# Five more pairs with seven products, other lead lengths, and sums of x beside the last latent heads in a hybrid encoder layer

## The chip, the cores and the metric

The kernel runs on one core of a Trainium2 chip. The metric is the device time of one launch in microseconds (us), given as the median of the runs. All engines of the core run side by side, each through its own instructions in order: TensorE (PE, matmuls, with weight loads as PEld), VectorE (DVE), ScalarE (ACT), GpSimd (POOL) and SyncE (SP), which issues most of the DMA transfers. Semaphores order them against each other.

## What is computed

One layer of a bidirectional encoder for 256 tokens of width 4096, in float32:

```python
h = rms_norm(x, g_mix)
c_q, c_kv, k_rope, gate_a, q_b, k_b, v_b, gate_b = split(h @ w_in)      # w_in: 4096 x 11840
# group A: latent attention, 16 heads, from c_q and c_kv (w_uq, w_ukv, rotary part)
# group B: dilated attention, 16 heads of 128, three (window, dilation) patterns
y_a = rms_norm(mla(...), g_out_mla) * silu(gate_a)
y_b = rms_norm(dilated(q_b, k_b, v_b), g_out_dil) * silu(gate_b)
x = x + concat([y_a, y_b]) @ w_out                                      # 4096 x 4096
x = x + (p @ w_ple) * sigmoid(rms_norm(x, g_ple) @ w_ple_gate)          # 256 x 4096, 4096 x 4096
out = rms_norm(x, g_final)
```

Nearly all of the work is the products with w_in, w_out and w_ple_gate, whose rows are read from HBM once each.

## The kernel before

**Products in three matmuls.** A float32 number is split into a high part (`hi`, written by ACT, L115) and the rest (`lo`, written by DVE, L116, after ACT). A product of a 128x128 block of activations with 512 columns of weights is three matmuls: high by high, high by low, low by high (L133 to L135). The activations are split beforehand; the weights are split as they arrive.

**Blocks, plain steps and pairs.** A `Block` (L781) multiplies the 256 tokens (two tiles of 128) with 1024 columns of a weight matrix of 4096 rows, that is 32 blocks of 128 rows. A *plain step* takes one block of rows: one load of 512 KB, one split of 1024 columns, and four products (two token tiles by two halves of 512 columns). A *pair* (`fast_steps`, L825) takes two blocks of rows, a 2x2 by 2x2 product of tiles, in seven products instead of eight: four steps "s" with 1, 2, 2 and 2 products. For this it needs sums of activation tiles (made beforehand by `add_sums`, L865, and flagged one pair at a time: five sums on DVE and a split for each pair) and sums of weight tiles, four subtractions of 512 columns each, on DVE (L833) beside the splits. `half_way` and `all_way`, or the `_mid` and `_done` tasks of a block, put the products together, the former after the last step of the last pair.

**The order of a block.** `weave(fast, lead, trail)` (L1187) writes the order as a string: `lead` plain steps ("c"), then the pairs with the remaining plain steps spread among them (at most so many in front of the pair and one between its first and second step), then `trail` plain steps. `lay` (L1203) puts them on the list of steps.

**Tiles and their ring.** A converted step lives in a tile of `hi` and `lo`. Tiles are handed out in the order of the block's ring: three of the pool "wp" and one to three larger buffers that are free just then (`tiles`, L1421). Some buffers join only when a flag is up (`gated_rings`, L1249): B4 in (q,0) when gate 2 of the latent heads has been multiplied in. A step's tile comes free when the matmuls of its last user are done, so DVE and ACT can be ahead of PE by as many steps as the ring has tiles. `phase`, where given, sets the position in the ring at the first step of a block; before, only the first dilated block has it.

**Tasks beside the steps.** After each step, `advance` (one *tick*) runs each open task to its next `yield`: attention heads, norms, gates, sums. So a task with more yields is spread over more steps. Every engine runs what it was given in that order.

**Stages.** From the input projection: latents and the first gates of group A; the latent heads beside 64 steps; `ga3`, the last gate of group A (16 plain steps of two row blocks at 512 columns); six dilated blocks (q,0), (k,0), (v,0), (q,1), (k,1), (v,1); four dilated gates with the dilated heads beside them; three output blocks and two plain output parts; four wide blocks (w_ple_gate), the last of 2 x 384 columns; a last part of 256 columns.

**What the change touches.** `y_stats` (L557) adds up the heads' squares when all 16 heads of a branch are done, takes the root in `rsqrt_mean` (L225, three rounds, each behind a yield) and raises the flag that the gates wait for. The gates 0 to 3 follow each other. `x_sums` (L1277) makes the sums of x for the first seven pairs of the dilated blocks when the last latent head is done, into the tiles T0 to T5 and T7, which the heads have used (T0 and T1 hold queries and keys of even and odd heads, T2 and T3 their weights, T4 the scores); the eighth follows gate 3 (which lies in T6). `y_sums` (L923) makes seven sums of the heads' output; the seventh lies in T4. `load_res` (L722) reads the residual x for an output block on POOL's queue into T0 to T5, two parts per block. The wide blocks' end, `wide_done` (L1063), takes four quarters through tanh, gate, addition and squares, one after another; from the third of its six rounds on it leaves five ticks to the next in blocks 0 to 2, and one in block 3.

Of the kernel before, what the change touches and what calls it, by code (L numbers as in the profile page):

```python
# [20 lines left out]
NT = S // P  # L21
DM = 4096
HEADS = 16
# [55 lines left out]
def encoder_layer(ctx: ExitStack, tc: tile.TileContext, x, p, positions, g_mix, w_in, g_q_latent, w_uq,  # L79
# [329 lines left out]
    def attend(h, q_src, k_src, pe, v, y, dil):  # L409
# [15 lines left out]
        for t in range(NT):  # L425
            a = tuple(qk[:, i, t * P:(t + 1) * P] for i in range(2))
            b = tuple(qk[:, i, S:] for i in range(2))
            mm(s[:, t], a, b, True, pe is None)
            if pe is not None:
                both = pe[0]()[:, t * P:(t + 1) * P]  # L430
                nc.tensor.matmul(s[:, t], both, pe[1][0], start=False, stop=False)
                nc.tensor.matmul(s[:, t], both, pe[1][1], start=False, stop=True)
        yield
        i = h % 2
# [122 lines left out]
    def y_stats(dil):  # L557
# [6 lines left out]
        yield  # L564
        yield from rsqrt_mean(ry[dil], tp[:, :NT], WIDTH)
        nc.vector.tensor_tensor(ry[dil], ry[dil], rxh, op=ALU.mult)
# [496 lines left out]
    def wide_done(k, blk):  # L1063
# [10 lines left out]
        def task():  # L1074
# [7 lines left out]
            for n in range(6):  # L1082
# [6 lines left out]
                for i, t, h, m in quarters[n - 2:n - 1] if n > 1 else ():  # L1089
                    for u, xc, at, c in pieces(h, i):  # L1090
                        nc.scalar.activation(u, xc[:, t, at], AF.Square, accum_out=ss2[:, t, c:c + 1])
                for _ in range(5 if n > 1 and k < WIDE - 1 else 1):
                    yield
# [132 lines left out]
    def hook(at, f):  # L1226
        assert at not in hooks
        hooks[at] = f
# [30 lines left out]
    hook(len(steps), only("t0", "t1"))  # L1259
    M = M[::-1]  # L1260
    ga2 = from_x(OFF_GA + 1024, 512, done_gate(0, 2))
    other, ga2.banks = M
# [5 lines left out]
    hook(len(steps), lambda: spawn(y_stats(0)))  # L1268
    hook(len(steps) + 1, lambda: spawn(x_sums()))
    ga3 = from_x(OFF_GA + 1536, 512, done_gate(0, 3))  # L1270
# [6 lines left out]
    def x_sums():  # L1277
        while ("head", False, HEADS - 1) not in flags:
            yield
        z = lambda j: slot(z_tags[j], [2, 4, P], F32R)  # L1280
        yield from add_sums(7, x_pair, z, "B0", "x_sums", x_s)
# [5 lines left out]
    for n, key in enumerate((key, i) for i in range(2) for key in "qkv"):  # L1287
        off = {"q": OFF_Q, "k": OFF_K, "v": OFF_V}[key[0]] + 1024 * key[1]
        order = weave((range(5), range(8), range(8), range(8), (4, 5, 0, 1, 2, 3, 6, 7), (0, 1, 2, 3, 6, 7))[n],
                      16 if n == 0 else 2, 2)  # L1290
        ring = (["B6", "B4"], ["B4", "B6", "B0"], ["B4", "B6", "B0"], ["B4", "B6"], ["B4", ("T4", "T7")], [("T4", "T7")])[n]
        after = ((), (), ["B4", "B6"], ["B4"], [("T4", "T7")], ())[n]
        blk = Block(w_in[:, off:off + 1024], lhs_x, x_s, "x_sums", order, lambda kt: (), tags, "B1", WP + ring)
        lay(blk, order, d_mid(key, blk), d_done(key, blk), after=after, used={2: ("used", 5)} if n == 4 else {})
        if n == 0:
            steps[-len(order[1])].phase = 0
        tags = follow(tags)
# [9 lines left out]
    for k in range(WIDE_O):  # L1307
        hook(len(steps), only(*(("t0", "t1"), ("m2", "m3"), ("m0", "m1"))[k]))
        for h in range(2):
            hook(len(steps) + 4 + h, lambda c=2 * k + h: load_res(c))  # L1310
        order = weave(*((range(4), 12, 4), (range(7), 6, 4), (range(6), 8, 4))[k])
        blk = Block(w_out[:, 1024 * k:1024 * (k + 1)], lhs_y, y_s, "y_sums", order, lambda kt: need_y(kt // 2),
                    tags, "Al2" if k < 2 else "Al1", WP + (["Ah2", "Al1"] if k < 2 else [("B7b", "T7")]))
        lay(blk, order, out_mid(k, blk), out_done(k, blk))
        tags = follow(tags)
    for c in (6, 7):
# [5 lines left out]
    for k in range(WIDE):  # L1322
# [4 lines left out]
        if k == 3:  # L1327
            hook(len(steps), lambda: spawn(load_g()))
        lay(blk, order, wide_mid(k, blk), wide_done(k, blk), wide_ple(k, q), **({"after": [], "used": {4: "z used"}} if k == 3 else {}))
    small = Chunk(cols(w_ple, 3840, 256), 2, 256, lambda kt: (pT[0][:, 0, kt], pT[0][:, 1, kt]), ("t0", "t1"), done_p(8),  # L1330
                  lambda j: ["pT"])
# [236 lines left out]
```

## Time and profile before

| what | value |
|---|---|
| median of 3 runs | 1924.12 us (1924.05 to 1924.25) |
| the profiled execution, as listed | 1922.93 us |
| its span, first to last instruction | 1921.2 us |
| mean granted clock of PE | 0.998 |
| matmuls, weight loads | 9246 each |
| HBM read, written | 364.72 MB, 4.19 MB |
| 512 KB loads of w_in, w_out, w_ple_gate | 320, 128, 96 |

The profile's rows are read as follows. In a timeline: start in us from the span's start, duration, engine, line, operation, destination and sources by tile name with the number left out, shape, and the count of merged instructions; in brackets the idle time before it and what ended it. A matmul of the timeline is listed with its full duration although the next one starts before it ends, so rates are read from starts. In a table of stretches: start and end, length, then busy time and count by engine, granted clock of PE, DMA share and rate. A piece of the chain has start, length on the chain and what ran.

The places of the blocks in the trace come from counting: each product is three matmuls, and the steps' products in order give the first matmul of each block. (q,0) runs from 487.7 to 576.2 (its first pair from 535.2), (k,0) to 657.9, the output blocks from 1201.7, 1287.1 and 1371.4 to 1456.3, wide blocks 2 and 3 from 1725.1 and 1813.6 to 1885.2.

### The profile page before, as it was taken

To read this page: it belongs to the slowest core of one execution; us is meant where nothing else is said; L and a number is where in the kernel's file an instruction comes from. 1 tells how busy PE (TensorE), PEld (TensorE's weight loads), DVE (VectorE), ACT (ScalarE), POOL (GpSimd) and SP (SyncE) were. 2 spreads that over 40 slices of the span, in tenths; PEclk is the share of its full clock that TensorE was granted. 3 is DMA by queue.
4 is the path that set the end of the run, shared out by engine and by line. 5 is a ranking of instruction groups with operands and counts; after the bars stand their busy time and mean duration, and the time that the engine had idled before them with its cause. 6 is when DMAs were issued, how large, how long until landed. Compare 5 with 4: busy or idle time off the path is not lost.

```text
span 1921.2 us, 25661 instructions
## 1 busy us (share of the span) xinstructions
PE 1905.4 (99%) x9246; PEld 1629.2 (85%) x9246; DVE 1589.1 (83%) x2221; ACT 1114.5 (58%) x1547; POOL 71.3 (4%) x115
## 2 busy tenths in 40 slices
PE   9999999999999999999999999999999999999997
PEld 8998889998888888888888888888888888888897
DVE  7877966665999999899877778889896698989897
ACT  6655555565555565655556666555565455566554
POOL 0001011220000000000000010000000000000000
PEclk9999999999999999999999999999999999999999
DMA  7666654445656666666664456665666556566565
GB/s 260 196 181 198 206 164 145 143 153 157 196 186 206 212 209 197 214 200 196 213 195 143 132 165 219 204 213 172 233 195 217 188 190 218 183 212 202 190 220 195
DMA packets 139350, 370.58 MB, mean 193 GB/s; under 512 B 12476, under 2 KB 33816, under 8 KB 139224
## 3 DMA queue, kind: packets, MB, share of 16 engines
q1 hardware_dynamic: 137816, 363.96, 59.5%
q0 software_dynamic: 1408, 5.00, 0.7%
q8 instruction: 72, 1.18, 0.2%
q14 instruction: 54, 0.44, 0.1%
HBM read 364.72 MB, written 4.19 MB: 192 GB/s over the span
## 4 chain that ended last, share of the span: by engine, by line
PE 93%; DVE 5%; ACT 1%; issue 1%; DMA 1%; DVEq 0%; ACTq 0%
PE m L134 19%; PE m L135 19%; PE m L133 19%; PE t L133 4%; PE t L134 4%; PE t L135 4%; PE s L134 3%; PE s L135 3%; PE s L133 3%; PE o L134 3%; PE o L135 3%; PE o L133 3%; DVE lo L116 1%; DVE B L833 1%; ACT hi L115 1%
## 5 line engine op out<-in xcount | busy, mean ns | idle before, releaser
L116 DVE TENSOR_TENSOR lo<-raw,hi 128x1024 fp32r<-128x1024 f32 (+5 forms) x478 | 519.3, 1092 | 191.4 <-ACT hi L115 188.5
L115 ACT ACTIVATE hi<-raw 128x1024 fp32r<-128x1024 f32 (+5 forms) x478 | 454.0, 954 | 336.7 <-PE m L135 152.1
L133 PE MATMUL m<-hi,Ah 128*128 128x512 f32 (+3 forms) x1001 | 383.5, 383 | 0.0
L134 PE MATMUL m<-lo,Ah 128*128 128x512 f32 (+3 forms) x1001 | 378.3, 378 | 0.4 <-DVE lo L116 0.2
L135 PE MATMUL m<-hi,Al 128*128 128x512 f32 (+3 forms) x999 | 376.4, 377 | 0.0
L134 PEld LDWEIGHTS m<-lo,Ah 128*128 128x128 f32 x1001 | 188.5, 188 | 31.0 <-DVE lo L116 3.8
L135 PEld LDWEIGHTS m<-hi,Al 128*128 128x128 f32 x999 | 187.7, 188 | 31.3 <-DVE Al L127 0.7
L133 PEld LDWEIGHTS m<-hi,Ah 128*128 128x128 f32 x1001 | 188.4, 188 | 27.9 <-ACT hi L115 0.3
L133 PE MATMUL m<-hi,B 128*128 128x512 f32 (+2 forms) x429 | 163.6, 381 | 0.0
L134 PE MATMUL m<-lo,B 128*128 128x512 f32 (+2 forms) x429 | 159.9, 373 | 0.1
L135 PE MATMUL m<-hi,B 128*128 128x512 f32 (+2 forms) x429 | 159.9, 373 | 0.0
L115 ACT ACTIVATE hi<-B 128x1024 fp32r<-128x1024 f32 (+1 forms) x85 | 87.8, 1035 | 93.4 <-DVE B L833 55.2
L116 DVE TENSOR_TENSOR lo<-B,hi 128x1024 fp32r<-128x1024 f32 (+1 forms) x85 | 101.0, 1190 | 6.7 <-ACT hi L115 3.7
L833 DVE TENSOR_TENSOR B<-raw,B 128x512 f32<-128x512 f32 (+1 forms) x138 | 92.7, 671 | 0.0
L135 PEld LDWEIGHTS m<-hi,B 128*128 128x128 f32 x429 | 80.5, 188 | 11.8
L134 PEld LDWEIGHTS m<-lo,B 128*128 128x128 f32 x429 | 80.7, 188 | 11.1 <-DVE lo L116 0.6
L133 PEld LDWEIGHTS m<-hi,B 128*128 128x128 f32 x429 | 80.6, 188 | 10.5
L115 ACT ACTIVATE B<-raw 128x1024 fp32r<-128x1024 f32 (+2 forms) x68 | 61.4, 910 | 43.4 <-DMA raw<-in_w_in_dram 18.7
L115 ACT ACTIVATE B<-B 128x1024 fp32r<-128x1024 f32 (+2 forms) x62 | 59.2, 955 | 44.6 <-DVE B L833 23.8
L116 DVE TENSOR_TENSOR B<-raw,B 128x1024 fp32r<-128x1024 f32 (+2 forms) x68 | 70.2, 1038 | 11.0 <-ACT B L115 10.9
L848 DVE TENSOR_TENSOR lo<-raw,hi 128x1024 fp32r<-128x1024 f32 (+2 forms) x64 | 76.2, 1190 | 2.9 <-ACT hi L846 2.9
L116 DVE TENSOR_TENSOR T<-t,T 128x512 fp32r<-128x512 f32 x64 | 43.9, 687 | 41.6 <-ACT T L115 41.2
(769 smaller groups left out, 4020.3 us busy)
## 6 DMA issues: line engine op xcount, KB each, us to landing
raw<-in_w_in_dram SPq DMA_DIRECT2D x320, 512.0 KB, 4.0
raw<-in_w_out_dram SPq DMA_DIRECT2D x128, 512.0 KB, 4.5
raw<-in_w_ple_gate_dram SPq DMA_DIRECT2D x96, 512.0 KB, 4.6
raw<-in_w_in_dram SPq DMA_DIRECT2D x63, 400.0 KB, 3.7
raw<-in_w_uq_dram SPq DMA_DIRECT2D x32, 384.0 KB, 3.3
raw<-in_w_ple_gate_dram SPq DMA_DIRECT2D x32, 384.0 KB, 3.7
raw<-in_w_ukv_dram SPq DMA_DIRECT2D x16, 512.0 KB, 3.5
raw_l<-in_w_ple_gate_dram SPq DMA_DIRECT2D x8, 512.0 KB, 4.6
```

The source lines that it names most:

```text
L115: nc.scalar.activation(hi, src, AF.Copy)
L116: nc.vector.tensor_tensor(lo, src, plain(hi), op=ALU.subtract)
L133: nc.tensor.matmul(ps, ah, bh, start=start, stop=False)
L134: nc.tensor.matmul(ps, ah, bl, start=False, stop=False)
L135: nc.tensor.matmul(ps, al, bh, start=False, stop=stop)
L833: nc.vector.tensor_tensor(dst, a, b, op=ALU.subtract)
L848: nc.vector.tensor_tensor(lo, r[1], plain(hi), op=ALU.subtract)
```

## The change

Line numbers in the diff are those of the old kernel.

- (q,0) gets seven pairs instead of five, behind 12 plain steps instead of 16; the first output block six instead of four, behind 10 instead of 12; the third output block seven instead of six, behind 6 instead of 8, with pair 6 first.
- `x_sums` is started four steps before the end of the latent stage and waits for the scores of head 14 and the end of head 13, instead of the end of head 15.
- `y_stats` of the latent heads runs its root without yields.
- `wide_done` of wide block 2 leaves one tick after each round, as that of block 3 does.
- Every dilated, output and wide block gets a fixed position in its ring.

```diff
@@ attend
                 nc.tensor.matmul(s[:, t], both, pe[1][1], start=False, stop=True)
+        flags.add(("scored", dil, h))
         yield
@@ y_stats
-        yield from rsqrt_mean(ry[dil], tp[:, :NT], WIDTH)
+        for _ in rsqrt_mean(ry[dil], tp[:, :NT], WIDTH):
+            if dil:
+                yield
@@ wide_done
-                for _ in range(5 if n > 1 and k < WIDE - 1 else 1):
+                for _ in range(5 if n > 1 and k < WIDE - 2 else 1):
                     yield
@@ the steps of the latent heads
+    hook(len(steps) + 60, lambda: spawn(x_sums()))
     ga2 = from_x(OFF_GA + 1024, 512, done_gate(0, 2))
...
     hook(len(steps), lambda: spawn(y_stats(0)))
-    hook(len(steps) + 1, lambda: spawn(x_sums()))
@@ x_sums
-        while ("head", False, HEADS - 1) not in flags:
-            yield
+        while ("scored", False, HEADS - 2) not in flags or ("head", False, HEADS - 3) not in flags:
+            yield
+        yield
@@ the dilated blocks
-        order = weave((range(5), range(8), range(8), range(8), (4, 5, 0, 1, 2, 3, 6, 7), (0, 1, 2, 3, 6, 7))[n],
-                      16 if n == 0 else 2, 2)
+        order = weave((range(7), range(8), range(8), range(8), (4, 5, 0, 1, 2, 3, 6, 7), (0, 1, 2, 3, 6, 7))[n],
+                      12 if n == 0 else 2, 2)
...
-        if n == 0:
-            steps[-len(order[1])].phase = 0
+        steps[-len(order[1])].phase = (0, 0, 0, 1, 0, 2)[n]
@@ the output blocks
-        order = weave(*((range(4), 12, 4), (range(7), 6, 4), (range(6), 8, 4))[k])
+        order = weave(*((range(6), 10, 4), (range(7), 6, 4), ((6, 0, 1, 2, 3, 4, 5), 6, 4))[k])
...
+        steps[-len(order[1])].phase = k
@@ the wide blocks
+        steps[-len(order[1])].phase = 3 if k else 1
```

## The prediction

> **What bounds the kernel now.** I read the page first, then the matmuls in order of time, then VectorE (DVE) around each block that the change touches, because a matmul can start only when DVE has written the `lo` half of its weights.
>
> ```profile
> span 1921.2 us, 25661 instructions
> PE 1905.4 (99%) x9246; PEld 1629.2 (85%) x9246; DVE 1589.1 (83%) x2221; ACT 1114.5 (58%) x1547; POOL 71.3 (4%) x115
> ```
>
> ```profile
> 599.63 0.39 PE L134 MATMUL m<-lo,Ah 128*128 128x512 f32 x1
> ...
> 603.93 0.39 PE L135 MATMUL t<-B,T 128*128 128x512 f32 x1
> ```
>
> The matrix engine is the bound. The two timeline rows are the first and the last of 20 consecutive matmuls: 4.30 us over 19 steps is 0.2265 us each, less than the 0.39 us that each is shown to last, since they overlap. A product is three matmuls, 0.68 us; a plain step (four products) is 2.72 us; a pair (seven products) is 4.76 us, where the two plain steps that it replaces take 5.44 us.
>
> DVE is busy 83% on average, but the mean hides stretches in which it is the slower of the two.
>
> ```profile
> 443.00:487.70 44.70, 44.70 (x224) 37.77 (x223) 26.43 (x43) 21.92 (x35) 3.52 (x3) 1.00 0.55 168
> 535.20:576.20 41.00, 40.88 (x178) 32.97 (x177) 40.49 (x52) 24.48 (x28) 0.00 (x0) 1.00 0.61 192
> 576.20:657.90 81.70, 81.70 (x362) 67.63 (x362) 79.72 (x94) 47.54 (x52) 0.00 (x0) 1.00 0.67 213
> 1826.00:1885.20 59.20, 58.17 (x331) 56.23 (x330) 52.16 (x75) 36.23 (x53) 0.00 (x0) 1.00 0.70 228
> ```
>
> These are stretches, with their length, then busy time of PE, weight loads, DVE, ACT, POOL, then the granted clock and DMA. 535.2 to 576.2 is the first dilated block, (q,0), from its first pair to its end: 177 matmuls (five pairs, six plain steps) by 0.2265 is 40.1 us of 41.0, so PE lost about 0.9 us, with DVE busy 40.49.
>
> ```profile
> 526.10 0.68 DVE L833 TENSOR_TENSOR B<-raw 128x512 f32<-128x512 f32 x1
> ...
> 531.38 0.86 DVE L593 SCALAR_TENSOR_TENSOR B<-B,gT,t 128x256 f32<-128x256 f32 x2
> ...
> 535.25 0.68 DVE L833 TENSOR_TENSOR B<-raw 128x512 f32<-128x512 f32 x1
> ...
> 536.45 0.68 DVE L116 TENSOR_TENSOR B<-raw,B 128x512 fp32r<-128x512 f32 x1
> 537.05 0.68 DVE L871 TENSOR_TENSOR B<-Ah,Al 128x512 f32<-128x512 f32 x1
> 537.77 1.02 DVE L871 TENSOR_TENSOR B<-B 128x128 f32<-128x128 f32 x4
> 538.71 1.22 DVE L116 TENSOR_TENSOR B<-raw,B 128x1024 fp32r<-128x1024 f32 x1
> 539.85 0.68 DVE L116 TENSOR_TENSOR T<-B,T 128x512 fp32r<-128x512 f32 x1
> 540.45 0.68 DVE L833 TENSOR_TENSOR B<-raw,B 128x512 f32<-128x512 f32 x1
> ...
> 545.34 0.69 DVE L833 TENSOR_TENSOR B<-raw 128x512 f32<-128x512 f32 x1
> 545.95 0.69 DVE L833 TENSOR_TENSOR B<-raw,raw 128x512 f32<-128x512 f32 x1
> 546.55 1.82 DVE L116 TENSOR_TENSOR B<-raw,B 128x512 fp32r<-128x512 f32 x2
> 548.29 0.68 DVE L833 TENSOR_TENSOR B<-raw,B 128x512 f32<-128x512 f32 x1
> 548.89 1.22 DVE L848 TENSOR_TENSOR lo<-raw,hi 128x1024 fp32r<-128x1024 f32 x1
> ...
> 550.63 2.52 DVE L116 TENSOR_TENSOR lo<-B,hi 128x1024 fp32r<-128x1024 f32 x2
> 553.18 0.69 DVE L833 TENSOR_TENSOR B<-raw 128x512 f32<-128x512 f32 x1
> ```
>
> From 545.34 to 553.18 DVE works without a pause on one pair and the plain step woven into it: 7.84 us, against 4.76 + 2.72 = 7.48 us of PE. The plain step's part is the 1024-wide `lo`, 1.14 us from start to start (538.71 to 539.85). So **a pair alone costs DVE 6.70 us and PE 4.76 us.** Each pair with a plain step inside eats 0.36 us of the cover (the time by which DVE is ahead), each pair without one 1.94 us.
>
> ```profile
> 523.19 0.48 PE L133 MATMUL m<-hi,Ah 128*128 128x512 f32 x1
> ...
> 535.20 0.39 PE L133 MATMUL m<-B,Ah 128*128 128x512 f32 x1
> ...
> 539.96 0.39 PE L133 MATMUL m<-B,Ah 128*128 128x512 f32 x1
> ...
> 555.81 0.39 PE L133 MATMUL m<-B,Ah 128*128 128x512 f32 x1
> 556.27 0.50 PE L134 MATMUL m<-B,Ah 128*128 128x512 f32 x1
> ```
>
> DVE began the first pair at 526.10, PE at 535.20. For the second pair the cover is already small (DVE turns to it at 535.25 and has its first `lo` by 536.45 + 0.68 = 537.13; PE comes at 539.96: 2.8 us), and it is gone by the fourth, where a matmul starts 0.46 us after its predecessor instead of 0.23.
>
> **The change, part by part.** *Removed.* Five pairs drop one product each: 15 matmuls by 0.2265 is **-3.40 us**, two pairs each in (q,0) and in the first output block, one in the third. That is what can be won where PE never waits.
>
> *(q,0).* The weave string by its own rule: 12 plain steps, then seven pairs with only four plain steps among them, at pairs 2, 4, 6 and 7; before it was 16, then five pairs with four, at pairs 2 to 5. Pairs 3 and 5 stand bare. DVE's account from the second pair on: four pairs with a plain step lose 4 by 0.36 = 1.44, two bare ones 2 by 1.94 = 3.88. The eighth sum of x, which waits for the last gate, stays in this stretch: 537.05 to 538.71 and 0.60 for its split, 2.26 us. The last gate's products are two bursts like 531.38, 0.79 each; one of them still falls behind the first pair. Together 1.44 + 3.88 + 2.26 + 0.79 = 8.4 us. Against it stands the cover. Before, the fifth tile B4 was released to the ring (its condition is gate 2) just as the first pair asked; now the gate comes three ticks earlier, since the root is no longer spread, but the first pair asks four steps earlier, and gets four tiles. Its fourth step must wait until the step before the pairs has left B6, at 523.19, then take a `hi`, a `lo` and the next pair's 1.8 us: some 527.4, with PE there at 523.19 + 4.76 = 527.95, or about 0.3 later with transposes. I put the cover at 0.8. PE then loses 7.6 us where it lost 0.9: +6.7. From this I take off 0.7 because the transposes of gates 1 and 2 move ahead of the pairs and hold PE there: **+6.0 us**. The ends: with the fifth tile in time (cover 2.8) and the gate hidden, 5.3 + 2.3 - 2.8 = 4.8 of loss, with the eighth sum hidden as well 2.5, so +1.6; with no cover, all 8.4 and a microsecond in the block behind it, +8.5.
>
> *First output block.* Six pairs, each with one plain step, behind 10 steps instead of 12.
>
> ```profile
> 1244.28 1.22 DVE L116 TENSOR_TENSOR lo<-raw,hi 128x1024 fp32r<-128x1024 f32 x1 [0.60 <-ACT hi L115]
> ```
>
> ```profile
> 1249.06 0.39 PE L133 MATMUL m<-hi,B 128*128 128x512 f32 x1
> ```
>
> The plain step of the second pair is converted by 1245.50 and run at 1249.06: a cover of 3.6 us, with DVE waiting for tiles. Five more pairs at 0.36 leave 1.8. **0 us**; up to +1.0 if the seventh sum of y falls on a later pair than the first.
>
> *Third output block.* Seven pairs behind six steps, on a ring of four.
>
> ```profile
> 1401.25 1.22 DVE L116 TENSOR_TENSOR lo<-raw,hi 128x1024 fp32r<-128x1024 f32 x1 [0.47 <-ACT hi L115]
> ```
>
> ```profile
> 1403.31 0.39 PE L133 MATMUL m<-hi,B 128*128 128x512 f32 x1
> ```
>
> Here the cover in the second pair is 0.84 us. Before, the third pair had a second plain step that refilled it; now pairs 3 to 6 have one each and lose 1.44: **+0.6 us** (0 to +1.5, as the pairs begin two steps nearer to the turning of the block before). Pair 6 goes first because its sums lie in T4, which the residual's load must have:
>
> ```profile
> 1360.31 1.44 POOL L724 DMA_DIRECT2D T<-in_x_dram  x2 [200.18 <-PE o L135]
> ```
>
> Both loads waited on POOL's queue for the last use of pair 6, in the second output block. Now they wait until about step 10 of the third, some 37 us later; only the load for T5 is queued behind, and the tiles are first used when the last pair ends, some 40 us after that. 0 us; with pair 6 last, out_mid would wait for the load.
>
> *Last wide block.* The work after wide block 2 (tanh, gate, add, squares) is no longer spread over five ticks a quarter.
>
> ```profile
> 1836.61 0.68 DVE L1086 SCALAR_TENSOR_TENSOR B<-B,T 128x512 f32<-128x512 f32 x1
> 1837.33 0.69 DVE L1088 TENSOR_TENSOR T<-B,T 128x512 f32<-128x512 f32 x1
> ```
>
> ```profile
> 1836.82 0.33 PE L133 MATMUL t<-hi,B 128*128 128x384 f32 x1
> ...
> 1837.86 0.34 PE L133 MATMUL m<-B,Ah 128*128 128x384 f32 x1
> 1838.95 0.45 PE L134 MATMUL m<-B,Ah 128*128 128x384 f32 x1 [0.75 <-DVE B L116]
> ```
>
> The last quarter takes DVE 1.33 us in the middle of the pairs, and PE starts its next matmul 1.09 us after the last one, 0.9 late. Moved into the plain steps ahead, this and the quarter before it (as long) leave the pairs; the lead has little idle, so I credit **-1.0 us**. The ends: all that is late in 1826 to 1885 (331 matmuls by 0.173, the distance over the six from 1836.82 to 1837.86, is 57.4 of 59.2), -1.8; and +0.5, if ACT's four tanh and four squares delay the `hi` of the first pair.
>
> *Sums of x.* Seven by 2.26 is 15.8 us of DVE, moved some eight steps forward into 443 to 487.7, where DVE idles 18.3 us of 44.7. The heads hold T0 to T4 only until their scores and transposes, which are asked before. **0 us** (-0.2 to +1.0; with the cover gone, PE's transposes for the last heads wait). The flag costs no instruction, and y's root is the same instructions in one burst. The fixed ring phases are, by counting steps, where each block's ring stood before: 0 us, 0.3 either way.
>
> *Sum.* -3.40 + 6.0 + 0 + 0.6 - 1.0 = **+2.2 us**, made against the span of 1921.2. That execution is listed at 1922.93; the median of the runs is 1924.12, and the same 2.2 on it gives 1926.3.
>
> **Rivals.**
> *A. DVE keeps up.* If (q,0) loses no more than it did, the change gives -3.4 - 1.0 = -4.4: 1919.7. For it: the second output block now runs seven pairs without a long gap. Against: those all have plain steps within. It decides at 7.6 us of cover at the second pair; the largest that I see there is 2.8.
> *B. The debt is carried on.* If (k,0) starts with DVE behind, its own pairs stall too, and the upper end of (q,0), +8.5, holds with +0.6: 8.5 + 0.6 - 3.4 = +5.7, 1929.8. For it: (q,0) ends without cover and its results are still to be written. Against: it ended so before, too, and (k,0), 576.2 to 657.9, lost nothing (360 matmuls by 0.2265 are 81.5 of 81.7).
> *C. The sums do not move.* If their slots T0 to T4 come free late, they end where they did, inside the new first pair: one more sum, +2.3, is +4.5, 1928.6. The 18.3 us of idle speak against.
> *D. The clock.* The first warm-up matmuls are slow:
>
> ```profile
> 1.46 3.17 PE m L1490 x7
> ```
>
> 3.17 / 7 is 0.453 us, twice 0.2265, so half speed exists; the granted clock in (q,0) is 1.00. If each of three long stalls were followed by as long a slow spell, half of 3.17 is lost each time: +4.8 more, +7.0, 1931.1. The Trainium skill ("TensorE: Matmul & The Clock Gate", section "A second HAM failure mode: psum-queue depth-cycling") says that frequent short idling between groups of matmuls can make the gate swing between half and full rate. By that rule the time would be D's; the trace agrees so far only in that the two rates exist.
>
> **How the numbers follow.** Forecast 0.51 (its own range 1923.5 to 1928.5), A 0.16, B 0.20, C 0.09, D 0.04. What a measurement of this kernel can tell from no change is 0.2%, 3.85 us: below 1920.3 or above 1928.0. Faster: half of A and little of the forecast, 0.10. Slower: B, D, half of C and 0.08 of the forecast, 0.37. Same: the rest, 0.53. The range goes from 1921.0 (the low end of (q,0) with the rest as taken, -3.4 + 1.6 + 0.6 - 1.0 = -2.2, and a microsecond for out-block and wide block) to 1930.0 (B).
>
> **What would show it.** In the changed trace: matmuls of (q,0) that start late at the bare pairs, some 2 us at each, 7 us in all, with DVE busy throughout; none late in the first output block; a few tenths in the third; the pause near the end of wide block 3 gone; the sums of x before 487. It is wrong if (q,0) from its first pair on loses under 3 us, or if ga3 or (k,0) stall.

## The result and the profile after

The changed kernel takes 1931.76 us (median of 6 runs, 1930.45 to 1932.30) where the kernel before takes 1924.18 (6 runs). The ratio is 1.0038, 95% interval 1.0026 to 1.0051: slower by 7.6 us. The forecast was 1926.3 in a range of 1921.0 to 1930.0, so the sign of the forecast's sum was right and its size was not.

The profiled execution is listed at 1931.67 us and has a span of 1929.9 us, 8.7 more than before. First the page of the changed kernel: span, busy times, and the shares of the chain that ended last.

```profile
span 1929.9 us, 25678 instructions
...
PE 1907.2 (99%) x9231; PEld 1624.3 (84%) x9231; DVE 1611.3 (83%) x2251; ACT 1119.5 (58%) x1557; POOL 73.2 (4%) x115
...
PE 81%; DVE 12%; DMA 3%; ACT 2%; issue 2%; SPq 0%; ACTq 0%; DVEq 0%
```

And the same line of the chain for the kernel before:

```profile
PE 93%; DVE 5%; ACT 1%; issue 1%; DMA 1%; DVEq 0%; ACTq 0%
```

The 15 matmuls are gone (9231 against 9246), and yet the time grew: the chain has lost twelve points of PE and gained seven of DVE, two of DMA and one each of ACT and issue. Where that happened is read from the lengths of the blocks, from a block's first matmul to the next block's first, counted as described above. The last column is what the forecast had for the block, removed matmuls included.

| stretch | before, us | after, us | difference | forecast |
|---|---|---|---|---|
| start to ga3 | 435.56 | 436.04 | +0.47 | 0 |
| ga3 | 52.15 | 52.37 | +0.22 | 0 |
| (q,0) | 88.55 | 93.75 | +5.20 | +4.64 |
| (k,0) | 81.62 | 82.03 | +0.41 | 0 |
| first output block | 85.45 | 84.88 | -0.57 | -1.36 |
| third output block | 84.95 | 87.01 | +2.06 | -0.08 |
| wide block 0 | 89.71 | 89.92 | +0.21 | 0 |
| last wide block | 71.63 | 72.23 | +0.60 | -1.0 |

These rows add up to +8.6 of the 8.7; every other stretch agrees within 0.1. The +0.47 at the start lies before anything that the change touches (the first of the moved sums of x starts at 456.58), and other kernels of this study with the same beginning show -0.48 to +0.63 there: it is run to run.

The stretches of the changed kernel that answer to those of before, with the columns as before (length, busy PE, weight loads, DVE, ACT, POOL, granted clock, DMA share, GB/s):

```profile
524.70:582.10 57.40, 53.44 (x223) 40.41 (x222) 55.56 (x70) 32.61 (x37) 0.00 (x0) 1.00 0.53 165
...
1377.10:1464.10 87.00, 85.73 (x381) 69.39 (x380) 77.63 (x95) 50.93 (x65) 1.44 (x2) 1.00 0.59 200
```

```profile
1846.00:1866.00 20.00, 19.86 (x113) 19.04 (x112) 18.85 (x29) 11.66 (x16) 0.00 (x0) 1.00 0.68 207
1866.00:1886.00 20.00, 18.38 (x103) 17.48 (x102) 15.73 (x23) 10.87 (x16) 0.00 (x0) 1.00 0.83 265
```

In (q,0), from its first pair to its end, DVE is busy 55.6 of 57.4 us and PE is not: DVE is the bound there. PE's busy time counts the listed durations, so of a matmul that starts late it shows only a part; how much PE loses is read from starts. The last two rows are from the last wide block, which begins at 1821.7, 8.1 us later than before. The early pause, at 1838.95 before, would now stand at 1847.1. It is gone: in 1846 to 1866 PE idles 0.14 us, and no matmul from the block's start to 1854 starts late. In 1866 to 1886 PE idles 1.6 us. The clock is 1.00 in every row.

**(q,0) in detail.** Matmuls of the changed kernel, in order of time, around two of the late places, and under them DVE's row of work there:

```profile
524.88 0.49 PE L133 MATMUL m<-hi,Ah 128*128 128x512 f32 x1
...
528.19 0.39 PE L135 MATMUL t<-hi,T 128*128 128x512 f32 x1
529.94 0.47 PE L133 MATMUL t<-B,T 128*128 128x512 f32 x1 [1.36 <-DVE B L596]
...
540.35 0.40 PE L133 MATMUL m<-hi,Ah 128*128 128x512 f32 x1
541.53 0.50 PE L134 MATMUL m<-lo,Ah 128*128 128x512 f32 x1 [0.78 <-DVE lo L851]
```

```profile
489.20 0.69 DVE L874 TENSOR_TENSOR B<-Ah,Al 128x512 f32<-128x512 f32 x1
...
496.06 0.69 DVE L874 TENSOR_TENSOR B<-Ah,Al 128x512 f32<-128x512 f32 x1
...
527.12 0.69 DVE L836 TENSOR_TENSOR B<-raw 128x512 f32<-128x512 f32 x1
527.73 0.69 DVE L836 TENSOR_TENSOR B<-raw,raw 128x512 f32<-128x512 f32 x1
528.33 0.69 DVE L116 TENSOR_TENSOR B<-raw,B 128x512 fp32r<-128x512 f32 x1
528.93 0.87 DVE L596 SCALAR_TENSOR_TENSOR B<-B,gT,t 128x256 f32<-128x256 f32 x2
...
530.85 0.69 DVE L874 TENSOR_TENSOR B<-Ah,Al 128x512 f32<-128x512 f32 x1
```

A matmul usually starts 0.23 us after the one before. At 529.94 it starts 1.75 after: the product writes the PSUM bank t, which still holds the transposes of the last gate, and the gate's multiplication (L596), which empties it, stands on DVE behind three operations of the second pair. At 541.53 a bare pair waits 0.95 us longer than usual for a `lo` (L851). Of the sums of x (L874) the sixth and seventh start at 489.20 and 496.06, in the plain steps of (q,0), the other five earlier, from 456.58 on; the eighth follows at 530.85, inside the first pair.

**Third output block.** Timeline of the changed kernel, all engines, and the piece of the chain of waits that led to it:

```profile
1402.77 1.44 POOL L727 DMA_DIRECT2D T<-in_x_dram  x2 [236.29 <-PE m L135]
...
1410.50 1.06 ACT L115 ACTIVATE B7b<-raw 128x1024 fp32r<-128x1024 f32 x1 [3.23 <-DMA raw<-in_w_out_dram]
...
1411.59 1.23 DVE L116 TENSOR_TENSOR T<-raw,B7b 128x1024 fp32r<-128x1024 f32 x1 [2.06 <-ACT B7b L115]
```

```profile
1402.86 7.26 DMA raw<-in_w_out_dram
```

```profile
1411.61 0.50 PE L133 MATMUL m<-B7b,B 128*128 128x512 f32 x1 [0.30 <-ACT B7b L115]
1412.87 0.50 PE L134 MATMUL m<-T,B 128*128 128x512 f32 x1 [0.76 <-DVE T L116]
```

The two residual loads go out at 1402.77 to 1404.2. A weight load started at 1402.86 takes 7.26 us, ACT waits 3.2 us for it and DVE 2.1 for ACT, and PE starts two matmuls 0.47 and 1.03 us late; no pair behind it refills the cover, and three more matmuls are 0.23 late. The transfers of 1400 to 1412, by issue (count, KB each, median us to landing), against those of the 20 us before:

```profile
raw<-in_w_out_dram SPq DMA_DIRECT2D x4, 512.0 KB, 7.3
T<-in_x_dram POOLq DMA_DIRECT2D x2, 512.0 KB, 8.3
```

```profile
raw<-in_w_out_dram SPq DMA_DIRECT2D x6, 512.0 KB, 4.5
```

**First output block.** The plain step inside the second pair, converted and run, and the seventh sum of y:

```profile
1236.16 0.69 DVE L874 TENSOR_TENSOR T<-B 128x512 f32<-128x512 f32 x1
...
1242.08 1.82 DVE L116 TENSOR_TENSOR lo<-raw,hi 128x512 fp32r<-128x512 f32 x2
```

```profile
1244.54 0.39 PE L133 MATMUL m<-hi,B 128*128 128x512 f32 x1
```

Converted by 1243.90 and run at 1244.54: the cover is 0.64 us, where the kernel before had 3.6. The seventh sum now starts as PE reaches the first pair, whose first matmul is counted at 1236.4. In the kernel before it was made at 1227.6, as the group of it there shows, and the first pair began at 1238.2, nearly four plain steps later:

```profile
L871 DVE TENSOR_TENSOR T<-B x1: 687/687/687, 1227.6 to 1227.6; 128x512 f32<-128x512 f32 x1
```

**Last wide block.** One row of ACT's timeline, PE's two late matmuls, and the end of wide block 2's last quarter on DVE, which came at 1838.0 before:

```profile
1873.86 0.84 ACT L115 ACTIVATE hi<-raw 128x768 fp32r<-128x768 f32 x1 [2.77 <-PE o L135]
```

```profile
1874.76 0.44 PE L133 MATMUL m<-hi,Ah 128*128 128x384 f32 x1 [1.00 <-ACT hi L115]
1875.75 0.44 PE L134 MATMUL m<-lo,Ah 128*128 128x384 f32 x1 [0.55 <-DVE lo L116]
```

```profile
1833.69 0.69 DVE L1091 TENSOR_TENSOR T<-B,T 128x512 f32<-128x512 f32 x1
```

The quarters are done by 1834.4, as PE reaches the first pair (1834.2), and no longer lie in the pairs. But at 1873.86 ACT has waited 2.8 us, and PE starts two matmuls 1.16 and 0.82 us late right after it (read from starts; the idle time in brackets is less, since a matmul is listed beyond the next one's usual start). What ACT waited for is put down to PE; the experiments below show that it was the weight tile.

### The profile page after: what moved, and what is told of

It reads as the page before. It is cut to its first block, busy times and chain, and to the rows that moved or that the text cites. A ratio compares the mean times of both kernels' runs of the same rounds, so it can differ in the third digit from the quotient of the medians.

```text
span 1929.9 us, 25678 instructions
## 1 busy us (share of the span) xinstructions
PE 1907.2 (99%) x9231; PEld 1624.3 (84%) x9231; DVE 1611.3 (83%) x2251; ACT 1119.5 (58%) x1557; POOL 73.2 (4%) x115
## 4 chain that ended last, share of the span: by engine, by line
PE 81%; DVE 12%; DMA 3%; ACT 2%; issue 2%; SPq 0%; ACTq 0%; DVEq 0%
PE m L134 17%; PE m L135 17%; PE m L133 17%; DVE lo L116 4%; PE t L133 4%; PE t L134 4%; PE t L135 4%; PE s L134 3%; PE s L133 3%; PE s L135 3%; PE o L134 3%; PE o L135 3%; PE o L133 3%; DVE B L836 2%; ACT hi L115 2%
## 5 line engine op out<-in xcount | busy, mean ns | idle before, releaser
L851 DVE TENSOR_TENSOR lo<-raw,hi 128x1024 fp32r<-128x1024 f32 (+2 forms) x62 | 73.9, 1192 | 3.9 <-ACT hi L849 3.9
L116 DVE TENSOR_TENSOR B<-raw,B 128x1024 fp32r<-128x1024 f32 (+2 forms) x64 | 66.2, 1038 | 11.9 <-ACT B L115 11.6
```

The source lines that it names most:

```text
L116: nc.vector.tensor_tensor(lo, src, plain(hi), op=ALU.subtract)
L851: nc.vector.tensor_tensor(lo, r[1], plain(hi), op=ALU.subtract)
```

## The experiments

Each edit is to the changed kernel. Where only one time was taken, the block lengths of its profile carry the verdict; they repeat within 0.1 us in blocks that nothing disturbs. Blocks without cover vary more: with the code of the change, the first output block takes 84.8 to 85.5 us in the profiles of this study, and the third 86.3 to 87.2.

**e1: (q,0) as before.**

```diff
-        order = weave((range(7), range(8), range(8), range(8), (4, 5, 0, 1, 2, 3, 6, 7), (0, 1, 2, 3, 6, 7))[n],
-                      12 if n == 0 else 2, 2)
+        order = weave((range(5), range(8), range(8), range(8), (4, 5, 0, 1, 2, 3, 6, 7), (0, 1, 2, 3, 6, 7))[n],
+                      16 if n == 0 else 2, 2)
```

> The changed kernel with (q,0) as it was: five pairs behind 16 plain steps, all else changed. By block lengths between first matmuls, (q,0) grew from 88.55 to 93.75 us with the change. If the pairs themselves are the cause (DVE's shortfall), (q,0) comes back to 88 to 89 us and the span falls by about 5 us, so the time is some 1926.5. If the earlier sums of x or the burst root are the cause, (q,0) stays above 91 us with five pairs too.

1924.64 us (10 runs) against 1923.71, ratio 1.0004 (0.9995 to 1.0013). (q,0) takes 87.61 us, a little below the 88 to 89 expected, and (k,0) 81.60. So the two further pairs cost 6.1 us in (q,0), and 0.4 in (k,0); what is left of the change there, the early sums of x and the root in one burst (not separated here), saves 0.94 against before and costs 0.2 in ga3.

**e5: narrow sums of weights in (q,0).** The four subtractions of 512 columns in a pair go over 64 columns, so the sums of weights are right in the first 64 columns alone.

```diff
+            w = 64 if narrow else self.q
...
-                sub(T[1][:, 0], r[1][:, 1], T[0][:, 0])
+                sub(T[1][:, 0, :w], r[1][:, 1, :w], T[0][:, 0, :w])
```

> The changed kernel, but the four subtractions of weight tiles of each pair of (q,0) cover 64 of their 512 columns (the rest of the tile is zero), so the products of (q,0) are not the layer's. Each pair then costs DVE about 4 by 0.45 us less, some 4.9 us against 4.76 of PE. DVE theory: the late matmuls of (q,0) vanish, its length falls from 93.75 to 86.5 to 88 us (18 plain steps and seven pairs are 82.3 us, transposes of the gates about 4). Rival, loads or the ring of tiles: the loads and the ring are the same, so (q,0) stays above 91.5 us.

1924.91 us (one run), (q,0) 86.83 us: 6.9 less than in the changed kernel, with the seven pairs in place. One late matmul is left, at the bank t, and shorter:

```profile
528.52 0.47 PE L133 MATMUL t<-B,T 128*128 128x512 f32 x1 [0.31 <-DVE B L596]
```

So DVE's work on the sums of weights makes 6.9 of the 7.7 us that PE loses from the first pair on (0.8 is left here), and most of the wait for the bank t is part of it: with less in front of it on DVE the gate's multiplication came at 527.51, not 528.93.

**e9: seven bare pairs behind 16 plain steps.**

```diff
-                      12 if n == 0 else 2, 2)
+                      16 if n == 0 else 2, 2)
```

> The changed kernel with the seven pairs of (q,0) behind 16 plain steps instead of 12, so all seven stand bare, and the gates' transposes are over before the first pair uses their banks t0 and t1. It separates DVE's account from the banks. Account: six bare pairs after the first lose 6 by 1.94 = 11.6 us, the eighth sum now falls behind 16 steps and before the pairs, the cover at the second pair is 2.8: 8.8 us late, (q,0) = 86.3 + 8.8 = about 95 us. Rival, that what is lost sits mostly in the early start and its banks: (q,0) falls below 92 us.

1933.59 us (one run), (q,0) 95.15 us and (k,0) 82.77. In the middle of the pairs, matmuls of the same place in two pairs that follow each other:

```profile
552.06 0.40 PE L133 MATMUL m<-hi,Ah 128*128 128x512 f32 x1
553.23 0.50 PE L134 MATMUL m<-lo,Ah 128*128 128x512 f32 x1 [0.77 <-DVE lo L851]
...
558.77 0.39 PE L133 MATMUL m<-hi,Ah 128*128 128x512 f32 x1
```

A bare pair takes 6.71 us, against 4.76 of its matmuls: 1.95 lost each time. The prediction's account of a pair on DVE was 6.70.

**e4: pairs further apart.** (q,0) with six pairs behind eight plain steps, the first output block with six behind eight, the third output block and wide block 2 as before.

```diff
-        order = weave((range(7), range(8), range(8), range(8), (4, 5, 0, 1, 2, 3, 6, 7), (0, 1, 2, 3, 6, 7))[n],
-                      12 if n == 0 else 2, 2)
+        order = weave((range(6), range(8), range(8), range(8), (4, 5, 0, 1, 2, 3, 6, 7), (0, 1, 2, 3, 6, 7))[n],
+                      8 if n == 0 else 2, 2)
...
-        order = weave(*((range(6), 10, 4), (range(7), 6, 4), ((6, 0, 1, 2, 3, 4, 5), 6, 4))[k])
+        order = weave(*((range(6), 8, 4), (range(7), 6, 4), (range(6), 8, 4))[k])
```

> A version to beat both: sums of x early as changed, (q,0) with six pairs behind 8 plain steps (ten plain steps among the pairs), the first output block with six pairs behind 8 steps (eight among them), third output block and the end of wide block 2 as before. DVE theory: with one or two plain steps in each pair its account is even, so (q,0) is 88.55 - 0.68 - 0.9 = 87.0 us, the first output block 85.45 - 1.36 = 84.1 us, in all about -3 us against before, some 1921.2. Rival, that early pairs cost whatever their spacing: (q,0) stays at 88.5 us or more and the time at 1924 or above.

1934.88 us (5 runs), ratio 1.0056 (1.0043 to 1.0070), (q,0) 98.53 us. The theory of spacing fell; the rival has the direction (88.5 us or more), but neither had the cause. The matmuls of (q,0), and the stretches around them:

```profile
518.59 0.40 PE L135 MATMUL m<-B,T 128*128 128x512 f32 x1
521.62 0.77 PE L133 MATMUL t<-B,T 128*128 128x512 f32 x1 [2.64 <-DVE B L596]
522.18 0.63 PE L134 MATMUL t<-B,T 128*128 128x512 f32 x1
522.61 0.63 PE L135 MATMUL t<-B,T 128*128 128x512 f32 x1
...
528.86 0.77 PE L133 MATMUL t<-hi,T 128*128 128x512 f32 x1 [4.77 <-DVE B L596]
```

```profile
520.00:530.00 10.00, 3.62 (x10) 2.69 (x11) 5.82 (x10) 2.00 (x2) 0.00 (x0) 0.55 0.59 178
530.00:540.00 10.00, 10.00 (x36) 8.01 (x35) 5.75 (x10) 4.20 (x5) 0.00 (x0) 0.77 0.08 31
```

The pairs begin before the gates are done, and each gate's transposes use the same banks t as the products of a pair. PE stops for 2.6 and for 4.8 us until DVE reaches the gate, and DVE reaches it late because of the pair. The wait at 529.94 in the changed kernel is the small form of the same thing. With these gaps the granted clock falls to 0.55 in the mean of 520 to 530, and the matmuls at 522.18 and 522.61 start 0.43 us apart.

**e2: no residual loads for the third output block.** The two parts of x that are loaded in its first half are set to zero instead, so the residual is left out of 1024 columns.

```diff
-        nc.gpsimd.dma_start(x1[c], x[:, 512 * c:512 * (c + 1)].rearrange("(t p) k -> p t k", p=P))
+        if c in (4, 5):
+            nc.gpsimd.memset(x1[c], 0.0)
+        else:
+            nc.gpsimd.dma_start(x1[c], x[:, 512 * c:512 * (c + 1)].rearrange("(t p) k -> p t k", p=P))
```

> The changed kernel, but the two residual parts of the third output block are set to zero on POOL instead of being loaded, with the same wait for pair 6; the residual is missing from 1024 columns. The third output block grew from 84.95 to 87.01 us, with a raw tile of w_out that was 3.2 us late just after those loads began. Theory that the 1 MB of residual, now moved into the pairs, collides with the weight loads: that wait goes, the block falls to about 85.0 us (still four pairs at 0.36 without cover). Rival, that seven dense pairs ask for weights faster than they come: the late raw tile and 87 us stay.

1929.86 us (one run), third output block 84.85 us, 2.16 less than in the changed kernel and 0.10 less than before, with the weave of the change. Its weight loads between 1400 and 1412:

```profile
raw<-in_w_out_dram SPq DMA_DIRECT2D x5, 512.0 KB, 4.6
```

4.6 us to landing instead of 7.3, and one matmul late on PE, by 0.19. So the collision with the residual is all that the forecast missed in this block: without it the block is 0.10 below the kernel before, where the forecast had 0.08, the removed product less 0.6 for cover.

**e3: the end of wide block 2 spread again.**

```diff
-                for _ in range(5 if n > 1 and k < WIDE - 2 else 1):
+                for _ in range(5 if n > 1 and k < WIDE - 1 else 1):
```

> The changed kernel with the end of wide block 2 spread over five ticks again. With the change the last wide block took 72.23 us instead of 71.63: the pauses at its third and fourth pair were gone, and one of 2 us came near its end. If the two are one account (what is saved early is waited for at the end), the block stays within 71.5 to 72.7 us, with the early pauses back and the late one gone. If the tighter end of wide block 2 is a loss of its own, the block is 71.6 or less; if it is a gain that other things hide, 73.5.

1932.02 us (one run), last wide block 73.38 us, 1.15 more than in the changed kernel: matmuls at 1846.0 and 1854.9 are late again by 0.65 and 0.51. The late pause is there in both (here at 1875.1 and 1876.1, by 1.02 and 0.82). So the tight end saves about what was forecast, 1.0, and the pause is something else.

**e8: no gain loads.** The eight loads of the gains of the last norm, 256 KB each, are replaced by ones.

```diff
-            nc.sync.dma_start(g_cols(512 * c), g_final[512 * c:512 * (c + 1)].unsqueeze(0).to_broadcast([P, 512]))
+            nc.gpsimd.memset(g_cols(512 * c), 1.0)
```

> The changed kernel with the eight loads of the last gain (2 MB written, on SP's queue between the weight loads of the last wide block) replaced by ones written on POOL; the last gain is missing from the output. Theory that these loads make the weight tiles late: the 2 us pause near the end of the last wide block goes, the block falls from 72.23 to 70 to 70.8 us. Rival, that the weight tiles are late because their buffers come free late: it stays above 71.5.

1929.30 us (one run), last wide block 69.66 us, 2.57 less, no late pause. The weight loads issued from 1855 to 1880, first in the changed kernel, then here (count, issue time min/median/max in ns, first and last start; then time to landing):

```profile
L812 SPq DMA_DIRECT2D raw<-in_w_ple_gate_dram x8: 328/328/1599, 1856.3 to 1877.3; - x8
...
DMA to landing us min/median/max: 3.9/4.6/8.2
```

```profile
L812 SPq DMA_DIRECT2D raw<-in_w_ple_gate_dram x10: 327/328/328, 1856.3 to 1879.8; - x10
...
DMA to landing us min/median/max: 3.1/3.7/4.6
```

With the gain loads a weight load takes up to 8.2 us and its issue up to 1.6; without them 4.6 and 0.33. Whether the queue or the transfer engines make it late, the next run tells.

**e12: gain loads on GpSimd's queue.**

```diff
-            nc.sync.dma_start(g_cols(512 * c), g_final[512 * c:512 * (c + 1)].unsqueeze(0).to_broadcast([P, 512]))
+            nc.gpsimd.dma_start(g_cols(512 * c), g_final[512 * c:512 * (c + 1)].unsqueeze(0).to_broadcast([P, 512]))
```

> The changed kernel with the gain loads on GpSimd's queue in place of SyncE's. Theory (a weight load waits behind the gain loads on SyncE's queue): no ACT-released pause in the second half of the last wide block, block 69.7 us against 72.2, the rest as the changed kernel, about 1929.3. Rival (what is shared is the transfer engines, not the queue): pause still there, block 71.5 to 72.5, 1931 to 1932.

1936.39 us (one run), last wide block 77.39 us: far worse than both expected. The weight loads, two matmuls, and the stretches there:

```profile
L812 SPq DMA_DIRECT2D raw<-in_w_ple_gate_dram x7: 327/328/328, 1855.8 to 1879.6; - x7
...
DMA to landing us min/median/max: 5.2/8.9/9.8
```

```profile
1869.83 0.44 PE L134 MATMUL m<-lo,Ah 128*128 128x384 f32 x1 [2.13 <-DVE lo L116]
1870.11 0.34 PE L135 MATMUL m<-hi,Al 128*128 128x384 f32 x1
1872.76 0.69 PE L133 MATMUL m<-hi,Ah 128*128 128x384 f32 x1 [2.31 <-ACT hi L115]
```

```profile
1870.50:1873.00 2.50, 0.24 (x1) 0.24 (x1) 0.26 (x1) 1.14 (x2) 0.00 (x0) 0.62 0.86 337
1873.00:1876.00 3.00, 2.69 (x8) 2.29 (x9) 3.00 (x5) 1.56 (x3) 0.00 (x0) 0.50 0.48 142
```

The issue of a weight load is quick again (0.33), so SyncE's queue is free, and yet a load takes 8.9 us in the median: the transfers themselves compete. On SyncE the eight gain loads started between 1862.8 and 1872.8, in line with the weight loads; on GpSimd's queue seven of them started within 3.7 us, from 1859.05 on, and took 9.9 us to landing in the median. Whether the other queue or the closer and earlier starts do the harm is not separated. The Trainium skill ("DMA: Bandwidth & Descriptors", section "Issuing engines are not separate DMA queues") states that transfers started by different engines run on the same 16 DMA engines and interleave; the run agrees, 8.9 us on two queues against 4.6 on one.

**e6: the gains alone.** Early sums and burst, five pairs in the first output block behind 12 steps, all else as before (the fixed ring positions stay).

```diff
-        order = weave((range(7), range(8), range(8), range(8), (4, 5, 0, 1, 2, 3, 6, 7), (0, 1, 2, 3, 6, 7))[n],
-                      12 if n == 0 else 2, 2)
+        order = weave((range(5), range(8), range(8), range(8), (4, 5, 0, 1, 2, 3, 6, 7), (0, 1, 2, 3, 6, 7))[n],
+                      16 if n == 0 else 2, 2)
...
-        order = weave(*((range(6), 10, 4), (range(7), 6, 4), ((6, 0, 1, 2, 3, 4, 5), 6, 4))[k])
+        order = weave(*((range(5), 12, 4), (range(7), 6, 4), (range(6), 8, 4))[k])
...
-                for _ in range(5 if n > 1 and k < WIDE - 2 else 1):
+                for _ in range(5 if n > 1 and k < WIDE - 1 else 1):
```

> A version to beat both: early sums of x and the burst root as changed, (q,0) with five pairs behind 16 steps, the first output block with five pairs behind 12 (each with one plain step, the last with two), third output block and the end of wide block 2 as before. From the run with (q,0) undone: (q,0) 87.6 instead of 88.55 us; first output block 85.45 - 0.68 = 84.8 us, as its cover after the first pair is 0.6 to 1.1 us and four pairs lose 1.1 to 1.4; the rest as before. In all -1.6 us against before, 0.08%, at the edge of what five rounds can tell. Rival, that the earlier sums cost as much elsewhere: the time is that of before.

1922.57 us (11 runs) against 1924.06, ratio 0.9992 (0.9983 to 1.0001): not clearly faster. The first output block takes 84.77 us, its 0.68 of three matmuls saved; the second gives 0.83 back, since a weight load of its first pairs comes late (6.6 us) and the transposes that add the residual (L744) start 0.69 late. That this follows from the five pairs is not shown: with six pairs in the first output block, e5 and e8 lose 0.40 and 0.59 at the same place, the other runs nothing.

**e10 and e11: the same with the tight end, the gain loads on GpSimd's queue.** e10 has the output blocks as before, e11 five pairs in the first. To the edits of (q,0) as in e6 and of the gain loads as in e12 comes, in e10 and then in e11:

```diff
-        order = weave(*((range(6), 10, 4), (range(7), 6, 4), ((6, 0, 1, 2, 3, 4, 5), 6, 4))[k])
+        order = weave(*((range(4), 12, 4), (range(7), 6, 4), (range(6), 8, 4))[k])
```

```diff
-        order = weave(*((range(6), 10, 4), (range(7), 6, 4), ((6, 0, 1, 2, 3, 4, 5), 6, 4))[k])
+        order = weave(*((range(5), 12, 4), (range(7), 6, 4), (range(6), 8, 4))[k])
```

> The kernel before, with three things of the change kept: the sums of x beside the last latent heads, the root in one burst, and the tight end of wide block 2; and one thing added: the gain loads go out on GpSimd's queue, not on SyncE's. All three output blocks and (q,0) are as before. Theory (the gain loads make the last block's weight tile late): (q,0) about 87.6 us (-0.9 against before), ga3 +0.2, last wide block 69.7 as where the loads were left out (-1.9), the output blocks as before: 2.6 us below the kernel before, about 1921.5. Rival (the eight 256 KB transfers slow the weight tile from whichever queue they come): last wide block 71 to 72.5 with the pause near its second half still there, 0.5 to 1.5 below the kernel before.

> As the run before it, and the first output block has five pairs behind twelve plain steps, so one product less than before there. Theory: first output block 84.8 us (-0.7 against before), and, if the second output block's 85.1 of the earlier run with this weave follows from it, +0.8 there, so no gain over the run before it; if that was run to run, the second block is 84.3 and the whole is 0.7 us below the run before it, 3.3 below the kernel before.

e10: 1928.41 us (10 runs) against 1923.87, ratio 1.0025 (1.0015 to 1.0034); e11: 1927.77 (11 runs), 1.0021 (1.0012 to 1.0030), both far above the 1921.5 or so that was expected. (q,0) is as expected (87.60 and 87.61), the last wide block is e12's again (77.19 and 77.67). In e11 the first output block gains 0.68 and the second gives back 0.77, at the same place as in e6.

**e13: six of the gain loads later.** As e10, with the gain loads on SyncE again and this edit:

```diff
-        for c in (1, 4, 0, 2, 3, 5, 6, 7):
+        for c in EARLY:
             nc.sync.dma_start(g_cols(512 * c), g_final[512 * c:512 * (c + 1)].unsqueeze(0).to_broadcast([P, 512]))
...
                 nc.vector.tensor_tensor(x1[c][:, t], x1[c][:, t], g_cols(512 * c), op=ALU.mult)
+        for c in (0, 2, 3, 5, 6, 7):
+            nc.sync.dma_start(g_cols(512 * c), g_final[512 * c:512 * (c + 1)].unsqueeze(0).to_broadcast([P, 512]))
+            yield
```

> As e10_early_tight ((q,0) and the output blocks as before; early sums of x, root in one burst, tight end of wide block 2 kept), with the gain loads back on SyncE's queue, but six of the eight issued only after the two chunks that need their gains first have been multiplied (in the changed kernel at 1883.7 us of the trace). Theory (2 MB of gain loads compete with the weight tiles of the last wide block's second half): no pause near its second half, block 69.7 us as where the loads were left out (71.6 before), (q,0) 87.6, output blocks as before; if the tail does not pay, 2.6 us below the kernel before. Rival (the gains now compete with the eight 512 KB loads of the tail): the block is shorter by up to 1.9 but the stretch after it longer by as much, 0.5 to 1 us below the kernel before.

1921.72 us (11 runs) against 1923.71, ratio 0.9991 (0.9982 to 1.0000). The last wide block takes 69.45 us, as the theory said, 2.2 less than before. The stretch after it is 37.2 us where it was 35.9: PE's matmuls end 2.0 earlier than before and the last multiplications on DVE only 0.7, as the rival said. Before, the chain that ended last ran through PE's matmuls there; now it runs through two loads of the tail's weights, of 5.86 and 5.68 us, and the eight such loads land in 5.8 us in the median where they took 4.6. Wide block 2 is 0.40 longer, which stays open. By the medians this is the fastest kernel of the study, 2.0 us below the one before; the interval just touches no change.

## Why the forecast was too low

By the two profiles the forecast fell 6.5 us short (+2.2 against +8.7): 2.1 in the third output block, 1.6 in the last wide block, 0.8 in the first output block, 0.6 in (q,0), 0.8 in three small places and 0.5 at the start.

**The account of DVE in (q,0) was right.** The forecast had PE lose 7.6 us from the first pair on, where it lost 0.9 before. From the first pair (524.88) to (k,0) there are 73 products, 219 matmuls by 0.2265 or 49.6 us, in 57.3: 7.7 lost. That this is DVE's work is shown by e5, and the price of a bare pair by e9. The cover of 0.8 fits as well: DVE has the second pair's first `lo` at 528.33 + 0.69 = 529.02, and PE, but for the wait at the bank t, would come at 524.88 + 4.76 = 529.64 or a little later. What failed there is the credit of 0.7 for the transposes that move ahead of the pairs: the twelve plain steps lose 3.85 us, the sixteen before lost 4.0, so 0.15 came of it. And a part of the loss took a form that the forecast did not have: 1.5 of the 7.7 is the bank t, held by the last gate's transposes until DVE comes to the gate (e5, where the gate comes earlier, has 0.47 of it left, and e4 has it larger).

**Third output block: the residual loads, costed at 0.** This is the largest miss, 2.1 us. The forecast asked who is queued behind the two loads on POOL's queue and found only one more load; it did not ask what else is in transfer when they start. Moved from 1360 to 1402.8, they fall into the first pairs, where the cover is under a microsecond, and lengthen a weight load to 7.3 us. e2 shows that without them one matmul is late, by 0.19. With the loads gone the block stands where the forecast had it, 0.6 for cover included.

**Last wide block: -1.0 forecast, +0.60 measured.** The forecast's step was right (e3: the tight end saves 1.15 us; the early pause is gone). It was given back by a late weight tile behind the gain loads, 2.0 us of pause, at a place that the forecast did not look at. e8 shows that those loads cause it. What stays open is why the kernel before and e6 have no such pause in their profiles: the changed kernel, e1 to e5 and e9 have it, two matmuls late by 1.3 to 2.5 us together, whether the end is spread or not. The traces show one difference. A transfer of 16 KB of instructions starts within 0.6 us of the block's first gain load in these seven, and 3.6 and 2.2 us ahead of it in the kernel before and e6. That it is the cause is not shown.

**First output block: cover 3.6 taken for the second pair, 0.64 found.** The forecast read the cover from a kernel in which the seventh sum of y lies some four plain steps ahead of the first pair, and said that it may cost up to 1.0 if the sum falls on a later pair than the first. It fell into the first, and by the rows of before (2.26 with its split) that would be 2.3 of the 2.9 us of cover that are missing; no run moved the sum alone. The pairs also begin three plain steps earlier, not two: `weave` put a thirteenth plain step in front of the first pair before (36.5 us into the block, now 28.3). The loss is 0.8 in this profile, and 0.7 to 1.4 in the others with this code.

**Sums of x, (k,0), wide block 0: 0 forecast, +0.22, +0.41 and +0.21.** The 0.22 is there in every run with the early sums. Of the seven sums, two already lay before 487.7 (they started at 478.76 and 484.72), and five do now, so three moved out of (q,0), not seven; with five pairs they save 0.94 there together with the burst (e1), which the forecast had at 0. e1 and e5 (81.60 in both) show that the 0.41 comes with the seven pairs and DVE's debt: it is the beginning of rival B. The 0.21 is run to run: e3, e5, e8 and e12, with the same code up to there, take 89.71 as before.

**The rivals.** A (DVE keeps up) fell: DVE is busy 55.6 of 57.4 us. B (the debt is carried on) has its mechanism in (k,0) but not its size, 0.41; in e9, with all pairs bare, it is 1.15. C (the sums do not move) fell: the seventh starts at 496.06, 29 us ahead of the first pair. D (the clock) fell for this kernel, with pauses up to 1.5 us at a clock of 1.00 in (q,0) and the output and wide blocks; that its 1931.1 lies near the measured 1931.76 is chance. e4 shows that the mechanism exists.

**The signs.** Late matmuls at the bare pairs with DVE busy came, and so did the end of the early pause in the last wide block. Against the prediction, two matmuls of the first output block are late (0.22 and 0.19), the third block has 2.2 us of late matmuls instead of a few tenths, the sixth and seventh sum of x start after 487, and ga3 and (k,0), which were not to stall, lose 0.22 and 0.41.

**The range.** Its upper end is B's: (q,0) at its worst and the third output block at its forecast, the credit of the last wide block left out, and nothing for the other terms. The upper ends that the prediction gives for its terms (8.5, 1.0, 1.5, 0.5, 1.0 and 0.3, less 3.4) add up to +9.4, or 1933.5, so the bounds of the terms were not carried into the range. In the end (q,0) was near its forecast, and four other terms were off on the same side, by 0.8, 2.1, 1.6 and 0.8 in all (ga3, (k,0) and wide block 0). One of them, the residual loads, had no bound at all: with them the third block loses 2.7 us where its bound was 1.5.

## What to carry to other kernels

A saved product is worth its matmuls only where the engine that prepares the weights has time to spare; in (q,0) the account of that engine per step, with the cover at the first step, gave the loss to within a few tenths, in the change and in e9, and it was made from one profile. A load that is moved has to be costed by what is in transfer at its new place, and not only by what is queued behind it: 1 MB of residual beside a stretch without cover cost 2.1 us, and the gain loads did more harm from GpSimd's queue than from that of the weight loads. A cover read in the old kernel holds in the new one only if the tasks that lay ahead of it still lie ahead.

## What the runs showed of the hardware

- With a gap of PE of 2.64 us (e4), and with two of 2.13 and 2.31 us with two matmuls between them (e12), the granted clock fell: to 0.50 in e12 (1873 to 1876), and in e4 to a mean of 0.55 over ten microseconds and of 0.77 over the next ten, with a second gap of 4.77 us among them. Single pauses of up to 1.5 us did not lower it. The Trainium skill ("TensorE: Matmul & The Clock Gate", section "HAM oscillation — how this bites in real kernels") gives gaps of over about 3.4 us as the condition; here a single gap of 2.64 us was enough: the matmuls right behind it start 0.43 us apart.
- A weight load of 512 KB lands in 4.5 us in the median when it is alone with its like, in 7.3 us beside two loads of the same size from another queue; loads of 384 KB land in 3.7 us alone, 4.6 us (8.2 at most) beside the 2 MB of gain loads on the same queue, 8.9 us beside the same 2 MB on GpSimd's, started closer together.
